# HGRN level products by predicated copies, two affine maps on ScalarE, and a two-pass norm in a one-core hybrid trunk layer

## The chip, the cores and the metric

The kernel runs on one core of one Trainium2 chip. The metric is the device time of that core in microseconds (us). A core has TensorE (PE in the profile; PEld is its weight load), VectorE (DVE), ScalarE (ACT), GpSimd (POOL) and the DMA queues, most of them issued by SyncE (SP). Each engine works through its own instructions in a fixed order and waits on semaphores for the others.

## The reference, cut to what matters

One layer of a bidirectional trunk is computed for a prompt of 256 rows and a sample of 2048 rows, 1024 columns each:

```
h = rms_norm(x) * (1 + scale1) + shift1
r,k,v,w,a,g | xb,gb | q,f,iv,og = split(h @ w_in)          # three groups of heads
mix = [rwkv7(r,k,v,w,a,g), rglru(xb,gb), hgrn2(q,f,iv,og)]  # each forward and backward
x = x + gate1 * (mix @ w_out)
x = x + gate2 * (silu(conv3(h2 @ w_gate)) * (h2 @ w_up)) @ w_down,   h2 = modulated rms_norm(x)
```

Two parts bear on the change. RWKV-7 needs, for each direction, the decay `exp(-exp(-softplus(-wl) - 0.5))`, which the kernel gets as the exponential of a running sum of `-c * (tanh(wl/2) + 1)`, and the keys `k * (1 + (a - 1) * k_a)`. HGRN2 works in chunks of 64 rows and needs, in every chunk, the 64 x 64 matrix `att[t, s] = sum_k q_t k_s exp(b_t - b_s)`, for s up to t forward and for s from t on backward.

## The kernel before, in words

All 2304 rows are held transposed, in nine pieces of 256 rows (PC). A first phase, `dense1`, takes five sections (four of two pieces, then one of one). For each section it goes through 29 column blocks of `w_in`, and each block is 8 x 3 matmuls: operands are split in two fp32r parts, hi and lo (L370, L371), and `mm3` (L374 to L376) sums three of the four products. In section 0 the weights are split on the spot and kept in DRAM; later sections load them back.

The small work is written as generators in six lanes. After every half block the main loop advances each lane by a fixed rate: lane 0 takes the RWKV jobs (`rw_job`, 40 of them: 5 sections x 4 pairs of heads x 2 directions), lane 2 HGRN and RG-LRU jobs (`hg_job`, 9), lane 3 the norm of the next section (`norm1`) and, behind it, further columns of the modulation. Lane 3 is run at high priority. That gives an order and a priority to each instruction; when the program is built, a planner with its own idea of durations then lays out the order of each engine, and adds the semaphores. After that nothing is reordered. A second phase does the prompt's output projection and MLP while the last jobs run, a third the same for the sample, with the backward scans beside it.

`norm1` (L452) takes a section in blocks of 128 rows, 14 blocks for the four later sections: load a block (tile x, one buffer, shared with the modulation's columns), Square with a row sum on ScalarE (L460), a reciprocal root by thirteen small VectorE instructions (`rsqrt`, L189 to L202, on a 128 x 1 column of tile nss), scaling on VectorE (L463), eight transposes (L469), modulation (L473) and a store to DRAM.

`rw_job` (L535) gets the decay's logarithm from a tanh on ScalarE (L551) and an affine map on VectorE (L553), then a scan (L558). The second tanh (L562) gives `a`; L572 forms (tanh + 1) * kk from it, L573 maps it affinely in place with two per-partition scalars, and L574 multiplies by k. L567 and L568 are exponentials, L577 to L580 the four products that go out, and L581 copies the chunk's last decay (128 x 8).

`hg_job` (L842) builds att for eight chunk-heads as one tile A (128 x 512, tile hA): first the diagonal (L900), then for the block sizes 1, 2, 4, 8, 16 and 32 a product on TensorE into PSUM (two for size 2, so seven in all). The product is right only where its level's 0/1 mask holds. So VectorE multiplies it by the mask into tile hl, which has one buffer (L923), and GpSimd adds hl to A (L924). L928 and L933 move decays on for the next level. The masks of the levels and the diagonal do not overlap and together cover all 64 x 64 places.

Of the kernel before, what the change touches and what calls it, by code (L numbers as in the profile page):

```python
# [10 lines left out]
F32 = mybir.dt.float32  # L11
# [90 lines left out]
def build(tc, a, o):  # L102
# [36 lines left out]
    eps = cst.tile([128, 4], F32, name="eps")  # L139
    for i, v in enumerate((RMS_EPS, GN_EPS, 1e-12, 0.0)):  # L140
        V.memset(eps[:, i:i + 1], v)
# [249 lines left out]
    def mt(tag, shape=(128, PC), bufs=1, dt=F32):  # L391
        return mp.tile(list(shape), dt, tag=tag, bufs=bufs, name=tag)
# [59 lines left out]
    def norm1(sec, n, xpool, xb):  # L452

        for b in range(2 * n):
            c = cond_of(sec + b // 2)
            ss = mt("nss", (128, 3), 2)
            x = xpool.tile([128, 1024], F32, tag="x", bufs=xb, name="x")
            SY.dma_start(x, xrows(None, sec * PC + b * 128, 128))
            jk = hp.tile([128, 1024], BF16, tag="hx", bufs=HXB, name="jk")
            S.activation(jk, x, AF.Square, accum_out=ss[:, 0:1])  # L460
            yield
            rsqrt(ss[:, 1:2], ss[:, 0:1], ss[:, 2:3], 1.0 / 1024, RMS_EPS)
            V.tensor_scalar_mul(x, x, ss[:, 1:2])  # L463
            yield
            for k4 in range(2):
                pt = ps("mm", [128, 4, 128], 2)
                for i in range(4):
                    k = 4 * k4 + i
                    T.transpose(pt[:, i, :], x[:, k * 128:k * 128 + 128], ident)  # L469
                hx = hp.tile([128, 4, 128], F32, tag="hx", bufs=HXB, name="hx")  # L470
                for i in range(4):
                    k = 4 * k4 + i
                    V.tensor_scalar(hx[:, i, :], pt[:, i, :], A1[:, k, c:c + 1], mod[:, k, c:c + 1],  # L473
                                    op0=ALU.mult, op1=ALU.add)
                SY.dma_start(dH[SI[sec]][4 * k4:4 * k4 + 4, :, b * 128:b * 128 + 128].rearrange("k p t -> p k t"), hx)
                yield
        h32s[sec] = True
# [57 lines left out]
    def rw_job(sec, n, p, d):  # L535
# [16 lines left out]
        yield  # L552
        V.tensor_scalar(th, th, -HALF_C, -HALF_C, op0=ALU.mult, op1=ALU.add)  # L553
        B = mt("t2", (128, 512))[:, :W]
# [17 lines left out]
        V.scalar_tensor_tensor(na, ta, 1.0, kk, op0=ALU.add, op1=ALU.mult)  # L572
        V.tensor_scalar(ta, ta, kah[:, p:p + 1], ka1[:, p:p + 1], op0=ALU.mult, op1=ALU.add)  # L573
        V.tensor_tensor(ta, ta, k, op=ALU.mult)  # L574
# [5 lines left out]
        V.tensor_tensor(AR[:, :, 1, :], c3(r), in_, op=ALU.mult)  # L580
        V.tensor_copy(WC[d][si][:, :, p:p + 1], ep[:, :, 64:65] if d == 0 else ep[:, :, 0:1])  # L581
        yield
# [260 lines left out]
    def hg_job(q, sec):  # L843
# [52 lines left out]
        A = mt("hA", (128, 8, 64))  # L896
        fA = A.rearrange("p c t -> p (c t)")
        G.tensor_tensor(j2(Ks), j2(Ks), qs, op=ALU.mult)
        pt = headsum(Ks)
        V.tensor_tensor(A, c8(pt), C[:, C_DG:C_DG + 64].unsqueeze(1).to_broadcast([128, 8, 64]), op=ALU.mult)  # L900
        yield
        for li, b in enumerate(LEVELS):
# [9 lines left out]
            else:  # L912
# [7 lines left out]
                terms = [(pt.rearrange("p c t -> p (c t)"), C_LV + 64 * li)]  # L920
            for pt, mo in terms:
                tl = mt("hl", (128, 8, 64))
                V.tensor_tensor(tl, c8(pt), C[:, mo:mo + 64].unsqueeze(1).to_broadcast([128, 8, 64]), op=ALU.mult)  # L923
                G.tensor_tensor(A, A, tl, op=ALU.add)  # L924
            gq = g[:, 0:2 * (Wg + 1)].rearrange("p (s r) -> p s r", s=2)[:, ::-1, 0:Wg:2]
# [867 lines left out]
```

## Time and profile before

| | |
|---|---|
| median of 3 runs | 4045.39 us (4037.32 to 4047.43) |
| profiled execution | 4042.86 us, of which the span from first to last instruction is 4041.1 us |
| mean granted TensorE clock | 0.949 of full speed |
| busy: PE, PEld | 3710.6 us (92%), 3095.8 us (77%) |
| busy: DVE, ACT, POOL | 2677.7 us (66%), 1483.4 us (37%), 1296.0 us (32%) |
| HBM | 472.69 MB read, 162.06 MB written, 157 GB/s over the span |

The page cuts the span into 40 slices. In the first fifteen, which are `dense1`, PE is busy 6 to 9 tenths and DVE 5 to 8; from slice 24 on PE is at 9 or more nearly throughout. In the groups below, a row gives busy microseconds, a mean in nanoseconds, and the idle time just before with what ended it; L numbers are lines of the kernel.

### The profile page before, as it was taken

The numbers are of one execution on the slowest core, as the hardware profiler recorded it, in microseconds if no ns is written. First come the engines' busy times: TensorE is split into PE (matmuls) and PEld (weight loads), VectorE is DVE, ScalarE is ACT, GpSimd is POOL, SyncE is SP. The second block draws the span as 40 slices with busy tenths as digits, with TensorE's granted clock in tenths as the row PEclk, the third lists the DMA queues.
The fourth block names the chain that finished last, engine by engine and source line by source line (L and its number), as shares of the span: only waits on it lengthen the run. The fifth ranks groups of instructions, "written<-read, shape, count | busy, mean of one in ns | idle before, by whom it ended". The sixth has DMA issues, their size and how long they took to land.

```text
span 4041.1 us, 75063 instructions
## 1 busy us (share of the span) xinstructions
PE 3710.6 (92%) x29752; PEld 3095.8 (77%) x29752; DVE 2677.7 (66%) x5203; ACT 1483.4 (37%) x2643; POOL 1296.0 (32%) x871
## 2 busy tenths in 40 slices
PE   6988999989999987799877999999989999999998
PEld 3766777767767775677765888888778999988998
DVE  5587888688668678966788754444764433376666
ACT  3445335334543545333333222222332222243333
POOL 2561132213023131233453333333333333333233
PEclk8999999989999887889999999999999999999999
DMA  7988977667776887654645322222512222242332
GB/s 243 300 253 247 273 206 231 223 197 224 245 213 204 256 258 216 195 159 145 187 129 175 108 85 84 76 78 71 170 57 78 70 64 63 63 141 79 91 93 84
DMA packets 766949, 639.69 MB, mean 158 GB/s; under 512 B 246970, under 2 KB 647686, under 8 KB 765574
## 3 DMA queue, kind: packets, MB, share of 16 engines
q1 hardware_dynamic: 734198, 600.66, 48.9%
q10 hardware_dynamic: 32400, 34.22, 2.7%
q8 instruction: 235, 3.85, 0.4%
q14 instruction: 116, 0.95, 0.1%
HBM read 472.69 MB, written 162.06 MB: 157 GB/s over the span
## 4 chain that ended last, share of the span: by engine, by line
PE 43%; DVE 9%; DMA 4%; issue 2%; POOL 1%; ACT 1%; SPq 0%; ACTq 0%; DVEq 0%; POOLq 0%
PE mm L374 6%; PE mm L376 5%; PE mm L375 5%; PE xh L374 5%; PE xh L376 5%; PE xh L375 5%; DVE raw L1452 1%; DVE x L1476 1%; PE e L374 1%; PE e L375 1%; DMA raw<-in_ffn_w_down 1%; DVE tm L1530 1%; PE e L376 1%; PE o L375 1%; PE o L374 1%
## 5 line engine op out<-in xcount | busy, mean ns | idle before, releaser
L371 POOL TENSOR_TENSOR wlo<-raw,whi 128x1024 fp32r<-128x1024 f32 x273 | 667.3, 2446 | 956.3 <-ACT whi L370 713.7
L374 PE MATMUL mm<-hhi,whi 128*128 128x512 f32 (+2 forms) x2224 | 815.6, 367 | 33.8 <-DVE hx L473 8.8
L375 PE MATMUL mm<-hlo,whi 128*128 128x512 f32 (+2 forms) x2224 | 802.0, 361 | 8.4 <-DVE hlo L293 5.6
L376 PE MATMUL mm<-hhi,wlo 128*128 128x512 f32 (+2 forms) x2224 | 798.7, 359 | 3.0 <-POOL wlo L371 3.0
L370 ACT CAST whi<-raw 128x1024 fp32r<-128x1024 f32 x333 | 348.7, 1048 | 739.2 <-PE mm L376 287.1
L374 PEld LDWEIGHTS mm<-hhi,whi 128*128 128x128 f32 x2224 | 438.0, 197 | 94.0 <-DVE hx L473 10.7
L375 PEld LDWEIGHTS mm<-hlo,whi 128*128 128x128 f32 x2224 | 438.7, 197 | 53.5 <-DVE hlo L293 6.4
L376 PEld LDWEIGHTS mm<-hhi,wlo 128*128 128x128 f32 x2224 | 437.9, 197 | 48.2 <-POOL wlo L371 3.8
L371 POOL TENSOR_TENSOR alo<-gs,ahi 128x384 fp32r<-128x384 f32 (+1 forms) x154 | 151.8, 986 | 439.3 <-ACT ahi L370 430.6
L374 PE MATMUL xh<-hhi,whi 128*128 128x384 f32 (+1 forms) x824 | 274.9, 334 | 4.0 <-ACT hhi L370 4.0
L375 PE MATMUL xh<-hlo,whi 128*128 128x384 f32 (+1 forms) x824 | 272.8, 331 | 5.3 <-DVE hlo L371 3.4
L376 PE MATMUL xh<-hhi,wlo 128*128 128x384 f32 (+1 forms) x824 | 273.5, 332 | 0.0
L1640 DVE SCALAR_TENSOR_TENSOR gs<-xh,vec,gs 128x378 f32<-128x378 f32 (+1 forms) x103 | 60.8, 590 | 313.6 <-ACT gs L1636 313.6
L1476 DVE TENSOR_TENSOR x<-mm,x 128x512 f32<-128x512 f32 x218 | 148.8, 686 | 109.9 <-PE mm L376 107.8
L1476 DVE TENSOR_TENSOR x<-xh,x 128x512 f32<-128x512 f32 x220 | 150.6, 686 | 76.5 <-PE xh L376 74.2
L1452 DVE TENSOR_TENSOR raw<-raw,g 128x1024 f32<-128x1024 f32 x98 | 133.0, 1358 | 72.3 <-DMA raw<-in_ffn_w_down 65.7
L1646 DVE SCALAR_TENSOR_TENSOR gs<-fsg,gs 128x384 f32<-128x384 f32 (+1 forms) x154 | 122.8, 797 | 62.5 <-ACT fsg L1645 62.2
L374 PEld LDWEIGHTS xh<-hhi,whi 128*128 128x128 f32 x824 | 156.3, 190 | 7.5 <-ACT hhi L370 4.6
L746 POOL COPY gm<-ar 64x256 f32<-64x256 f32 x120 | 57.4, 478 | 326.0 <-PE c L791 267.0
L375 PEld LDWEIGHTS xh<-hlo,whi 128*128 128x128 f32 x824 | 156.2, 190 | 7.5 <-DVE hlo L371 3.7
L376 PEld LDWEIGHTS xh<-hhi,wlo 128*128 128x128 f32 x824 | 156.4, 190 | 0.8
L924 POOL TENSOR_TENSOR hA<-hA,hl 128x512 f32<-128x512 f32 x63 | 101.0, 1602 | 171.6 <-DVE hl L923 167.9
(613 smaller groups left out, 8614.9 us busy)
## 6 DMA issues: line engine op xcount, KB each, us to landing
whi<-dW SPq DMA_DIRECT2D x116, 512.0 KB
wlo<-dW SPq DMA_DIRECT2D x116, 512.0 KB
raw<-in_ffn_w_gate SPq DMA_DIRECT2D x88, 512.0 KB
raw<-in_ffn_w_up SPq DMA_DIRECT2D x88, 512.0 KB
raw<-in_ffn_w_down SPq DMA_DIRECT2D x88, 512.0 KB
raw<-in_w_out SPq DMA_DIRECT2D x40, 512.0 KB
dAR<-AR SPq DMA_DIRECT2D x32, 512.0 KB
araw<-in_ada_w SPq DMA_DIRECT2D x32, 512.0 KB
```

The source lines that it names most:

```text
L370: S.copy(hi, raw)
L371: e.tensor_tensor(lo, raw, hi.bitcast(F32), op=ALU.subtract)
L374: T.matmul(out, whi, xhi, start=first, stop=False)
L375: T.matmul(out, whi, xlo, start=False, stop=False)
L376: T.matmul(out, wlo, xhi, start=False, stop=last)
L746: G.tensor_copy(gm[H[h], :, h, 0:64], ar[H[h], :, 0, :])
L924: G.tensor_tensor(A, A, tl, op=ALU.add)
L1452: V.tensor_tensor(raw, raw, g[f].unsqueeze(1).to_broadcast([128, 2, 512]), op=ALU.mult)
L1476: V.tensor_tensor(x1b[:, FS[f]], pt, x1b[:, FS[f]], op=ALU.add)
L1530: V.tensor_scalar(t[:, 128 * i:128 * i + 128], pt[:, 128 * i:128 * i + 128], A2[:, k, c:c + 1], mod[:, 24 + k, c:c + 1], op0=ALU.mult, op1 ...
L1640: V.scalar_tensor_tensor(gv[:, :, 1:rw], pv[:, :, 0:rw - 1], cw(0), gv[:, :, 1:rw], op0=ALU.mult, op1=ALU.add)
L1646: V.scalar_tensor_tensor(gs[:, :w], sg[:, :w], 1.0, gs[:, :w], op0=ALU.add, op1=ALU.mult)
```

## The change

Three edits, in three nested functions, and one constant column for a bias.

```diff
-    for i, v in enumerate((RMS_EPS, GN_EPS, 1e-12, 0.0)):
+    for i, v in enumerate((RMS_EPS, GN_EPS, 1e-12, -HALF_C)):
         V.memset(eps[:, i:i + 1], v)
...
     def norm1(sec, n, xpool, xb):
+        ss = mt("nss", (128, 3, 4), 1)
+        def rows(b):
+            x = xpool.tile([128, 1024], F32, tag="x", bufs=xb, name="x")
+            SY.dma_start(x, xrows(None, sec * PC + b * 128, 128))
+            return x
+        for b in range(2 * n):
+            x = rows(b)
+            jk = hp.tile([128, 1024], BF16, tag="hx", bufs=HXB, name="jk")
+            S.activation(jk, x, AF.Square, accum_out=ss[:, 0, b:b + 1])
+            yield
+        rsqrt(ss[:, 1, :2 * n], ss[:, 0, :2 * n], ss[:, 2, :2 * n], 1.0 / 1024, RMS_EPS)
         for b in range(2 * n):
             c = cond_of(sec + b // 2)
-            ss = mt("nss", (128, 3), 2)
-            x = xpool.tile([128, 1024], F32, tag="x", bufs=xb, name="x")
-            SY.dma_start(x, xrows(None, sec * PC + b * 128, 128))
-            jk = hp.tile([128, 1024], BF16, tag="hx", bufs=HXB, name="jk")
-            S.activation(jk, x, AF.Square, accum_out=ss[:, 0:1])
-            yield
-            rsqrt(ss[:, 1:2], ss[:, 0:1], ss[:, 2:3], 1.0 / 1024, RMS_EPS)
-            V.tensor_scalar_mul(x, x, ss[:, 1:2])
+            x = rows(b)
+            V.tensor_scalar_mul(x, x, ss[:, 1, b:b + 1])
             yield
...
-        V.tensor_scalar(th, th, -HALF_C, -HALF_C, op0=ALU.mult, op1=ALU.add)
+        S.activation(th, th, AF.Identity, scale=-HALF_C, bias=eps[:, 3:4])
...
-        V.tensor_scalar(ta, ta, kah[:, p:p + 1], ka1[:, p:p + 1], op0=ALU.mult, op1=ALU.add)
+        S.activation(ta, ta, AF.Identity, scale=kah[:, p:p + 1], bias=ka1[:, p:p + 1])
...
-        V.tensor_copy(WC[d][si][:, :, p:p + 1], ep[:, :, 64:65] if d == 0 else ep[:, :, 0:1])
+        S.copy(WC[d][si][:, :, p:p + 1], ep[:, :, 64:65] if d == 0 else ep[:, :, 0:1])
...
+        def put(pt, mo):
+            m = C[:, mo:mo + 64].bitcast(I32).unsqueeze(1).to_broadcast([128, 8, 64])
+            V.copy_predicated(A, m, c8(pt))
         G.tensor_tensor(j2(Ks), j2(Ks), qs, op=ALU.mult)
-        pt = headsum(Ks)
-        V.tensor_tensor(A, c8(pt), C[:, C_DG:C_DG + 64].unsqueeze(1).to_broadcast([128, 8, 64]), op=ALU.mult)
+        put(headsum(Ks), C_DG)
...
-            for pt, mo in terms:
-                tl = mt("hl", (128, 8, 64))
-                V.tensor_tensor(tl, c8(pt), C[:, mo:mo + 64].unsqueeze(1).to_broadcast([128, 8, 64]), op=ALU.mult)
-                G.tensor_tensor(A, A, tl, op=ALU.add)
+            for term in terms:
+                put(*term)
```

The diagonal and the seven products are now written straight into their places of A by VectorE, with the mask as predicate; there is no multiplication, no tile between and no addition. In `rw_job` the two affine maps and the small copy are ScalarE's. `norm1` loads the section's blocks once for the sums of squares, takes one reciprocal root for all (128 x 4), loads them a second time, and goes on as before. The number of times a job hands back to the main loop is the same in each.

## Rows read from the trace of the kernel before

**Rows 1.** Busy time by stage: PE, PEld, DVE, ACT, POOL, granted clock, DMA share, GB/s.
```profile
0.00:1500.00 1500.00, 1346.33 (x12847) 1029.10 (x12849) 1105.74 (x2369) 659.51 (x1227) 426.75 (x312) 0.94 0.78 238
1500.00:2200.00 700.00, 575.75 (x5897) 469.71 (x5891) 547.18 (x1061) 271.25 (x506) 241.60 (x170) 0.88 0.59 175
2200.00:4041.00 1841.00, 1788.49 (x11020) 1597.01 (x11016) 1024.82 (x1773) 552.60 (x912) 627.68 (x389) 0.98 0.29 87
```

**Rows 2.** Waits of PE in the first 1500 us: total, times, longest.
```profile
PE mm L267 <- DMA adaw<-in_ada_w: 15.0, 4, 5.4
PE x L587 <- DVE BK L577: 14.3, 9, 3.4
PE c L781 <- DVE uv L776: 9.1, 5, 3.0
PE mm L374 <- DVE hx L473: 8.8, 5, 3.0
...
PE mm L407 <- ACT araw L405: 6.7, 4, 2.4
```

**Rows 3.** Busy time in four slices of 100 us, columns as in Rows 1.
```profile
700.00:800.00 100.00, 95.49 (x888) 72.63 (x887) 61.95 (x150) 39.25 (x72) 17.21 (x18) 0.97 0.73 236
800.00:900.00 100.00, 81.67 (x789) 60.96 (x790) 85.39 (x201) 36.88 (x69) 20.57 (x17) 0.88 0.66 189
...
1000.00:1100.00 100.00, 95.95 (x950) 71.62 (x950) 72.99 (x175) 54.50 (x104) 7.70 (x11) 0.98 0.78 241
...
1200.00:1300.00 100.00, 92.06 (x955) 70.55 (x955) 84.48 (x175) 33.51 (x70) 35.06 (x24) 0.93 0.67 203
```

**Rows 4.** The masked products (L923) in two of these slices: DVE busy alone.
```profile
700.00:800.00 100.00, 0.00 (x0) 0.97 0.73 236
800.00:900.00 100.00, 4.76 (x7) 0.88 0.66 189
```

**Rows 5.** The chain's pieces around 1644 us: start, duration, what.
```profile
1644.04 0.43 PE mm L375
...
1645.93 0.23 PE mm L375
```

**Rows 6.** GpSimd's adds (L924) in the first 1500 us: POOL busy alone.
```profile
0.00:1500.00 1500.00, 100.95 (x63) 0.94 0.78 238
```

**Rows 7.** Timeline, three of these adds and VectorE beside them: start, duration, what.
```profile
208.53 1.87 POOL L924 TENSOR_TENSOR hA<-hA,hl 128x512 f32<-128x512 f32 x1 [3.98 <-DVE hl L923]
208.57 0.68 DVE L928 TENSOR_TENSOR hK<-hK,hg 128x512 f32<-128x512 f32 x1
...
212.67 1.75 POOL L924 TENSOR_TENSOR hA<-hA,hl 128x512 f32<-128x512 f32 x1
...
213.20 1.51 DVE L553 TENSOR_SCALAR t<-t 128x512 f32<-128x512 f32 x1
...
216.68 1.67 POOL L924 TENSOR_TENSOR hA<-hA,hl 128x512 f32<-128x512 f32 x1 [2.25 <-DVE hl L923]
...
217.11 1.79 DVE L578 TENSOR_TENSOR AR<-kk,ep 128x512 f32<-128x512 f32 x1
```

**Rows 8.** Two lines' instructions in ns: min, median, max.
```profile
L553 DVE TENSOR_SCALAR t<-t x40: 274/427/1506, 119.6 to 1593.1; 128x512 f32<-128x512 f32 x32, 128x256 f32<-128x256 f32 x8
L578 DVE TENSOR_TENSOR AR<-kk,ep x40: 408/692/1814, 124.8 to 1595.1; 128x512 f32<-128x512 f32 x32, 128x256 f32<-128x256 f32 x8
```

**Rows 9.** VectorE's groups that the change touches.
```profile
L923 DVE TENSOR_TENSOR hl<-xh,C 128x512 f32<-128x512 f32 x63 | 43.0, 683 | 24.4 <-PE xh L870 14.0 <-PE xh L919 7.6 <-POOL hA L924 2.4
L573 DVE TENSOR_SCALAR t<-t,kah,ka 128x512 f32<-128x512 f32 (+1 forms) x40 | 32.5, 813 | 0.4
L553 DVE TENSOR_SCALAR t<-t 128x512 f32<-128x512 f32 (+1 forms) x40 | 20.3, 507 | 38.6 <-ACT t L551 38.5
L581 DVE COPY WC<-ep 128x8 f32<-128x8 f32 (+1 forms) x40 | 11.4, 286 | 0.1
L463 DVE TENSOR_SCALAR x<-x,nss 128x1024 f32<-128x1024 f32 x14 | 10.5, 750 | 0.3
```

**Rows 10.** All work on the norm's statistics (tile nss): DVE busy.
```profile
0.00:1600.00 1600.00, 44.49 (x196) 0.93 0.77 237
```

**Rows 11.** ScalarE's groups nearest to the added instructions.
```profile
L562 ACT ACTIVATE t<-x,a0h 128x512 f32<-128x512 f32 (+1 forms) x40 | 25.5, 639 | 7.3 <-PE x L547 6.5 <-ACT t L568 0.7
L238 ACT ACTIVATE cth<-vec 128x8 f32<-128x8 f32 x2 | 0.3, 200 | 3.6 <-DVE vec L182 3.6
```

**Rows 12.** Waits of ScalarE in the first 1600 us: total, times, longest.
```profile
ACT ep L567 <- DVE t L558: 63.6, 32, 6.3
...
ACT jk L460 <- DMA x<-in_x_sample: 23.6, 8, 7.1
```

More of the change, by code (lines that the diff above doesn't have):

```diff
@@ L896, in hg_job @@
         A = mt("hA", (128, 8, 64))
-        fA = A.rearrange("p c t -> p (c t)")
+        def put(pt, mo):
+            m = C[:, mo:mo + 64].bitcast(I32).unsqueeze(1).to_broadcast([128, 8, 64])
+            V.copy_predicated(A, m, c8(pt))
         G.tensor_tensor(j2(Ks), j2(Ks), qs, op=ALU.mult)
-        pt = headsum(Ks)
-        V.tensor_tensor(A, c8(pt), C[:, C_DG:C_DG + 64].unsqueeze(1).to_broadcast([128, 8, 64]), op=ALU.mult)
+        put(headsum(Ks), C_DG)
         yield
```

## Prediction

> **What bounds the kernel now.** I read the stages first. From 2200 us on PE is busy 1788 of 1841 us at a granted clock of 0.98: that part is TensorE's, and nothing in the change reaches it. All the touched jobs run in the first 1600 us. There, up to 1500 us, PE is busy 1346 us, so it idles 154 us, and its clock is 0.94 [rows 1]. A clock below 1 means stretches at the lower of two rates: one matmul of mm3 follows another after 0.43 us at 1644 us and after 0.23 us at 1646 us, that is, at 1.2 and at 2.4 GHz [rows 5]; what PE did before is that it had just stood still for a weight split. At 0.94 the 1346 busy microseconds hold 0.06 x 1346 = 81 that full clock would save, so at most 154 + 81 = 235 us can be won in this stage, and a microsecond less of idling is worth up to 235 / 154 = 1.53.
>
> Then the waits of PE. Apart from the first loads (15.0 us) the longest three are on VectorE: 14.3 for the RWKV products, 9.1, and 8.8 for the norm's modulation; the longest on ScalarE is 6.7 [rows 2]. Each is short (2 to 3 us) and there are many: PE meets a result that is a little late, again and again. The reader should take from these rows that VectorE is what is late, though nothing there is one big hole.
>
> The slices say the same. Without HGRN products (700, 1000) DVE is busy 62.0 and 73.0, PE 95.5 and 96.0, clock 0.97 and 0.98. With them (800, 1200; seven products in slice 800 and none in 700 [rows 4]) DVE is busy 85.4 and 84.5, PE 81.7 and 92.1, clock 0.88 and 0.93 [rows 3]. Lost time of PE per slice, idle plus (1 - clock) x busy, is on average 6.7 us without and 13.1 + 0.095 x 86.9 = 21.4 us with. So 17.5 us more of DVE go with 14.7 us more lost: a slope of 0.84 (two slices against two, and HGRN brings more than DVE work, so it is an upper bound).
>
> **The change, part by part.**
>
> *Adds on GpSimd.* 63 adds go, 101 us of POOL, 1.60 us each [rows 6]. POOL itself is no bound (427 of 1500 us, rows 1). What counts is VectorE: an instruction that reads two SBUF operands, or a plain SBUF-to-SBUF map, that meets a GpSimd add runs on until the add is over. Of three adds in the timeline, the first came while VectorE was at work, and the add took the delay (1.87 us, the VectorE product its usual 0.68); the second stretched L553 to 1.51 us, the third L578 to 1.79 us [rows 7], against medians of 0.43 and 0.69 [rows 8]. That is (0 + 1.08 + 1.10) / 3 = 0.73 us of VectorE per add, 63 x 0.73 = 46 us. Bounds: none, or all 101 us.
> The Trainium skill says of this ("SBUF — State Buffer", SBUF: two separate sides) that whoever starts first takes the shared port pair for its whole instruction and the other fully blocks. The trace agrees in kind; read as if VectorE always lost, it would put the price at the upper end, 101 us, but in rows 7 the add is the one that waits in one case of three.
>
> *Products.* 63 masked products and 9 for the diagonal become 72 predicated copies with the same PSUM source and the same mask. A product takes 0.683 us [rows 9]. No predicated copy stands in the trace. It might take as long, or, if it works at half rate because it also has to mind what is in A, 2 x 0.683: between no change and 72 x 0.683 = +49 us; a gain of the same order can't be excluded by a row, but it reads no less. I take no change, since source, mask and output have the size of the nearest row. The copies of one A are in order on one engine, so what fell to the add (waiting for POOL's other work, and hl's single buffer, 2.4 us of VectorE waits) goes too.
>
> *Affine maps and copy.* VectorE loses L573 (32.5), L553 (20.3) and L581 (11.4): 64 us [rows 9]. ScalarE gains 80 maps; the nearest row, a tanh with a pointer bias over the same shapes, has 0.64 us, so 51 us, and 40 small copies at 0.20 make 8 [rows 11]: 59 us on 660 of 1500 [rows 1]. The first map follows a tanh on the same engine and only moves the hand-over to VectorE one step later (VectorE already waits there, 38.5 us in all [rows 9]). The second is worse: L573 stood between two VectorE instructions; now ScalarE waits for L572 (it overwrites what L572 reads) and L574 waits for ScalarE. Behind the waiting map stand, on ScalarE, the casts of L370 and the evacuations of mm; VectorE has L577's, L578's and L580's products to do meanwhile. The price as a wait lies between nothing and what the same job shows at its exponential, 63.6 us over 32 times, 2.0 us each [rows 12]. I take the low end for VectorE's side and charge ScalarE's side below.
> The Trainium skill ("ScalarE: Activation LUTs", Rules for kernel authors) would keep multiply-and-add on VectorE. By that page's figures (What ACT_TABLE_LOAD costs) I estimate 0.80 us for the map with two pointer operands and 0.71 for the other at 512 columns, which would make the 59 us some 65; on this kernel VectorE's own row, 813 ns for L573, shows no advantage left.
>
> *Norm.* 14 reciprocal roots become 4. Work on nss takes 44.5 us, of which 10.5 is the scaling [rows 9, 10]; 34 x 10/14 = 24 us go. (I take an instruction on 128 x 4 to be as short as one on 128 x 1; were it four times as long, nothing would be won here.) Added are 14 loads of 512 KB, 7.3 MB; at the stage's 238 GB/s that is 31 us of a DMA system that is busy 0.78 of the time [rows 1]. PE's waits on DMA end with the first loads [rows 2], so I count the loads as hidden by the matmuls; uncovered they would cost those 31 us. They queue on SP with the weights and the jobs' stores, 14 issues more. One thing turns: ScalarE's Square used to absorb the late block (23.6 us of waits, 8 times [rows 12]); in the second pass VectorE's scaling meets it. I charge 8 us to VectorE (a third; bounds 0 and 24). The norm is done well before its section needs it: the first pass adds four loads and Squares to it, some 4 x 8 us at the longest wait seen (7.1 us) plus a Square, in a section of some 300 us (1500 by five), which the slower lanes fill.
>
> *Sum.* VectorE: -46 - 64 - 24 + 8 = -126 us of 1106. From below, PE's idling shrinks in proportion to VectorE's busy time, 126/1106 of 154 = 18 us. From above, slope 0.84: 106 us. The two are far apart and I take their geometric middle, 44: the slope is inflated by HGRN's own chains, the proportion ignores that late results pile up and that idling costs clock as well. Against it ScalarE's 59 us (9% more): proportional to all of PE's idling 14 us; ScalarE ends fewer and shorter of these waits than VectorE [rows 2], so I take 5. Net -39. The profiled execution took 4042.9 us, so 4004; it lies 2.5 us under the median of 4045.4, and 4005 is what I write for the median to come.
>
> **The rivals.**
>
> *The gain stays hidden (about 4040).* PE's order was laid out once; if the waits on VectorE are mostly true dependences, as L587 after the last of a job's products, or if the 31 us of loads come out, the relief is idle time on VectorE. For it: each wait is short and PE waits for many lines. Against it: the slices with a quieter VectorE have PE at 95 to 96.
>
> *ScalarE becomes the late one (about 4070).* Forty second maps each stand at the head of ScalarE's queue until VectorE has done L572. With the exponential's 2.0 us and 0.64 us of work that holds ScalarE 40 x 2.64 = 106 us, and each evacuation behind it holds a PSUM buffer of mm. At the same slope of 0.84, 89 us if all of it reaches PE, 67 at three quarters; less the 44 won, that is +23 to +45, so 4066 to 4088. It decides from one half on, 0.84 x 53 = 44. For it: ScalarE's longest wait is of just this kind [rows 12]. Against it: mm has two buffers and a block takes some 10 us (29 in a section of about 300), so a hold of 2.6 us is mostly bridged.
>
> *All of the slope (about 3941).* VectorE's 126 us come out at 0.84, less ScalarE's 5. For it: slices 800 and 1000. Against it: 235 us is all there is, and part of it is loads at the start.
>
> *The planner's new order is worse by itself (some 4060).* Shorter jobs by its own durations move every engine's order in the first 2200 us; the second stage with its clock of 0.88 [rows 1] is the fragile one, and a few per cent of its 700 us are 20. Nothing in the rows speaks for a sign.
>
> **How the numbers follow.** Forecast, 3975 to 4032: 0.61. Whole slope: 0.09. Hidden: 0.18. ScalarE late: 0.08. Worse order: 0.04. A measurement of this kernel tells about 0.3%, 12 us, from no change. So faster 0.61 + 0.09 = 0.70, the same 0.18, slower 0.12. Copies at half rate would cost 49 x 44/126 = 17 us, still within the forecast (4022). The range goes from 3950, which leaves out most of the whole-slope case, to 4052, which leaves out the slower two.
>
> **What would show it.** Right: no add on GpSimd with tile hA; VectorE's busy time up to 1500 us near 980; L578, L580 and L928 seldom above 0.7 us; a predicated copy near 0.68 us; PE over 90 in the slices with HGRN, and clock above 0.95 in the stage. Wrong: a copy near 1.3 us; ScalarE's waits for L572 of more than 2 us each, with PE waiting for casts or evacuations; VectorE waiting for x loads for more than 24 us; or the first stage shorter while the second, up to 2200 us, takes it back.

## The result, and the profile after

The changed kernel takes 3988.98 us (median of 4 runs, 3979.92 to 3993.76) against 4042.61 us for the kernel before on the same chip: a ratio of 0.9865, 95% interval 0.9841 to 0.9889, or 54 us less. The forecast was 4005, in a range from 3950 to 4052. The profiled execution took 3979.92 us with a span of 3978.1, so it is the fastest of its runs, 63 us under the profiled execution of before.

The stages of after, to be laid beside [rows 1] (columns as there):

```profile
0.00:1500.00 1500.00, 1367.36 (x13588) 1049.63 (x13590) 1058.27 (x2263) 755.39 (x1426) 324.49 (x257) 0.96 0.82 253
1500.00:2200.00 700.00, 573.56 (x5496) 470.51 (x5493) 549.78 (x1056) 253.84 (x465) 258.64 (x177) 0.88 0.55 163
2200.00:4041.00 1841.00, 1735.35 (x10672) 1549.99 (x10671) 961.31 (x1637) 532.27 (x873) 607.83 (x374) 0.99 0.28 84
```

The first stage is denser (PE 1346 to 1367 busy at a clock of 0.96 instead of 0.94) and holds more of the work; the last only ends earlier. To see where the time was won, one needs a point of the work, not of the clock. I take the first gate product of the prompt's MLP on ScalarE, L1636 before and L1643 after. Times of these instructions in ns (min, median, max), then first and last start; before, then after:

```profile
L1636 ACT ACTIVATE gs<-mm,vec x8: 557/558/565, 1705.1 to 1843.3; 128x256 f32<-128x256 f32 x8
```
```profile
L1643 ACT ACTIVATE gs<-mm,vec x8: 558/560/567, 1643.8 to 1778.3; 128x256 f32<-128x256 f32 x8
```

So 61.3 of the 63 us are won before this point, called the gate from here on. Busy time up to the gate, before and after (columns as in [rows 1]):

```profile
0.00:1705.10 1705.10, 1498.27 (x14638) 1147.76 (x14639) 1279.96 (x2810) 754.31 (x1416) 460.41 (x343) 0.92 0.77 235
```
```profile
0.00:1643.80 1643.80, 1468.75 (x14583) 1126.58 (x14584) 1177.72 (x2544) 810.15 (x1531) 353.98 (x280) 0.93 0.81 248
```

VectorE is busy 102 us less, ScalarE 56 more, GpSimd 106 less. PE's idle time falls from 206.8 to 175.1 us (the stretch less its busy time), and its busy time falls by 29.5 us at a clock of 0.93 instead of 0.92: idling and the clock share the gain, roughly half and half (after shows 55 matmul records fewer before this point, worth some 5 us of the busy time). Behind the gate, where nothing was edited, the profiled execution of before takes 2336.0 us and that of after 2334.3.

The longest of PE's waits up to 1500 us (total, times, longest), for [rows 2]:

```profile
PE mm L267 <- DMA adaw<-in_ada_w: 16.2, 4, 5.0
PE x L552 <- ACT t L557: 11.5, 2, 10.8
PE mm L374 <- ACT whi L370: 7.9, 3, 3.7
PE e L761 <- DVE gm L755: 7.0, 3, 4.7
PE c L780 <- ACT mv L775: 6.5, 3, 3.2
```

The three waits on VectorE that stood behind the first loads (14.3, 9.1, 8.8) have left the top; one of 7.0 us is the longest left. Adding up the whole lists up to the gate, PE waits 37 us less for VectorE (114.7 before, 77.7 after), 11 us more for ScalarE (53.4, 64.1), and 2 us less for loads directly (25.6, 23.6). So the late results that went are VectorE's.

A wait on ScalarE has come in, most of it a single one of 10.8 us, on a tanh (L557). What ScalarE and VectorE did before it (start, duration, what, idle before and its releaser):

```profile
378.25 1.06 ACT L463 ACTIVATE jk<-x 128x1024 bf16<-128x1024 f32 x1 [8.20 <-DMA x<-in_x_sample]
...
383.18 0.23 DVE L1339 COPY hl<-hgS 128x128 f32<-128x128 f32 x1 [8.19 <-DMA dLA<-hl]
...
386.08 1.28 ACT L557 ACT_TABLE_LOAD   x1 [6.21 <-DVE nss L196]
...
388.11 0.79 PE L552 MATMUL x<-la,lrha 128*128 128x512 f32 x1 [10.83 <-ACT t L557]
```

The norm's Square waits 8.2 us for its rows, VectorE waits 8.2 us for a DMA that stores tile hl, and the tanh then waits for VectorE. So this wait goes back mostly to DMA, and not to the maps moved to ScalarE. Four slices of after, for [rows 3]:

```profile
700.00:800.00 100.00, 88.55 (x830) 66.28 (x827) 59.42 (x127) 34.12 (x63) 21.32 (x19) 0.90 0.67 214
800.00:900.00 100.00, 94.58 (x927) 71.59 (x927) 74.70 (x170) 43.31 (x83) 14.54 (x14) 0.91 0.76 219
...
1200.00:1300.00 100.00, 93.98 (x1139) 73.48 (x1136) 74.03 (x156) 45.13 (x93) 24.19 (x23) 0.96 0.78 228
...
1400.00:1500.00 100.00, 88.41 (x1269) 76.05 (x1267) 76.82 (x185) 62.79 (x134) 13.94 (x16) 0.94 0.86 276
```

In slices 800 and 1200 PE is at 94, where it had 82 and 92, with VectorE at 74 to 75 instead of 85. But HGRN's copies have moved too: slice 700, which had no product before, now holds four copies, as many as slice 800, and PE is at 88.6 there; slice 1400 holds eight, with PE at 88.4. So single slices do not show a size; the stage as a whole does.

VectorE's groups up to 1600 us (busy, mean ns, idle before and its releasers), for [rows 9], and two lines in ns (min, median, max), for [rows 8]; L584 is L578 of before:

```profile
L907 DVE COPY_PREDICATED hA<-C,xh 128x512 f32<-128x512 int32 x72 | 52.5, 730 | 24.0 <-PE xh L876 14.0 <-PE xh L928 9.4
...
L584 DVE TENSOR_TENSOR AR<-kk,ep 128x512 f32<-128x512 f32 (+1 forms) x40 | 25.9, 649 | 9.7 <-ACT ep L573 9.6
...
L469 DVE TENSOR_SCALAR x<-x,nss 128x1024 f32<-128x1024 f32 x14 | 12.6, 901 | 15.2 <-DMA x<-in_x_sample 15.1
```
```profile
L907 DVE COPY_PREDICATED hA<-C,xh x72: 708/728/751, 180.1 to 1437.6; 128x512 f32<-128x512 int32 x72
...
L584 DVE TENSOR_TENSOR AR<-kk,ep x40: 409/684/1366, 124.9 to 1535.2; 128x512 f32<-128x512 f32 x32, 128x256 f32<-128x256 f32 x8
```

The copy costs 0.73 us, hardly more than the product that it replaces. L584's maximum fell from 1814 to 1366 ns, but its neighbours still run to 2541 (L586) and 2774 ns (L585; L579 of before had 2007), so one line's maximum says little; the sum over all lines stands with the experiments. Work on the norm's statistics up to 1600 us, for [rows 10], fell from 44.5 to 21.3 us:

```profile
0.00:1600.00 1600.00, 21.28 (x66) 0.94 0.82 251
```

The new work on ScalarE, as groups, for [rows 11]:

```profile
L579 ACT ACTIVATE t<-t,ka,kah 128x512 f32<-128x512 f32 (+1 forms) x40 | 30.8, 771 | 25.4 <-DVE t L578 20.4 <-DVE ep L572 4.1 <-ACT mv L835 0.4
L559 ACT ACTIVATE t<-t,eps 128x512 f32<-128x512 f32 (+1 forms) x40 | 27.3, 681 | 2.7 <-DMA tt<-dTT 1.7
...
L587 ACT COPY WC<-ep 128x8 f32<-128x8 f32 (+1 forms) x40 | 7.9, 197 | 0.1
```

Together 66 us. For 512 columns the medians of L579 and L559 are 0.81 and 0.72 us. L579's wait for VectorE's L578 is the one that the ScalarE rival lived on; among ScalarE's waits up to 1600 us (total, times, longest) it stands like this, for [rows 12]:

```profile
ACT ep L573 <- DVE t L564: 49.3, 31, 6.8
...
ACT t L579 <- DVE t L578: 20.4, 15, 5.8
```

### The profile page after: what moved, and what is told of

It is laid out like the page before. It is cut to its first block, busy times and chain, and to the rows that moved or that the text cites. A ratio compares the mean times of both kernels' runs of the same rounds, so it can differ in the third digit from the quotient of the medians.

```text
span 3978.1 us, 74856 instructions
## 1 busy us (share of the span) xinstructions
PE 3676.3 (92%) x29752; PEld 3070.1 (77%) x29752; DVE 2569.4 (65%) x4953; ACT 1541.5 (39%) x2762; POOL 1191.0 (30%) x808
## 4 chain that ended last, share of the span: by engine, by line
PE 52%; DVE 14%; DMA 6%; ACT 3%; issue 3%; POOL 1%; SPq 1%; ACTq 0%; DVEq 0%; POOLq 0%
PE mm L374 7%; PE mm L376 7%; PE mm L375 7%; PE xh L374 6%; PE xh L375 5%; PE xh L376 5%; DVE raw L1459 2%; DVE x L1483 1%; DMA raw<-in_ffn_w_down 1%; DVE m L638 1%; DVE Dn L636 1%; PE e L374 1%; PE e L375 1%; PE e L376 1%; DVE tm L1537 1%
## 5 line engine op out<-in xcount | busy, mean ns | idle before, releaser
L371 POOL TENSOR_TENSOR wlo<-raw,whi 128x1024 fp32r<-128x1024 f32 x273 | 667.2, 2446 | 971.5 <-ACT whi L370 698.6
L374 PE MATMUL mm<-hhi,whi 128*128 128x512 f32 (+2 forms) x2224 | 798.6, 360 | 24.5 <-ACT whi L370 7.9
L375 PE MATMUL mm<-hlo,whi 128*128 128x512 f32 (+2 forms) x2224 | 785.4, 353 | 7.7 <-DVE hlo L293 5.6
L376 PE MATMUL mm<-hhi,wlo 128*128 128x512 f32 (+2 forms) x2224 | 784.9, 353 | 3.0 <-POOL wlo L371 1.8
L374 PEld LDWEIGHTS mm<-hhi,whi 128*128 128x128 f32 x2224 | 425.6, 192 | 83.8 <-issue 10.1
L375 PEld LDWEIGHTS mm<-hlo,whi 128*128 128x128 f32 x2224 | 426.2, 192 | 51.2 <-DVE hlo L293 6.3
L376 PEld LDWEIGHTS mm<-hhi,wlo 128*128 128x128 f32 x2224 | 426.0, 192 | 46.6 <-POOL wlo L371 3.0
L371 POOL TENSOR_TENSOR alo<-gs,ahi 128x384 fp32r<-128x384 f32 (+1 forms) x154 | 151.8, 986 | 419.5 <-ACT ahi L370 419.3
L371 POOL TENSOR_TENSOR t<-t,t 128x512 fp32r<-128x512 f32 (+1 forms) x40 | 52.9, 1323 | 359.7 <-ACT t L370 222.0
```

The lines of the kernel that those rows point to most:

```text
L371: e.tensor_tensor(lo, raw, hi.bitcast(F32), op=ALU.subtract)
L374: T.matmul(out, whi, xhi, start=first, stop=False)
L375: T.matmul(out, whi, xlo, start=False, stop=False)
L376: T.matmul(out, wlo, xhi, start=False, stop=last)
```

## The experiments

Theories that the expectations speak of. *VectorE*: the time comes from VectorE's shorter busy time, at one rate for all of it. *Chain*: it comes from A's chain over GpSimd (product, tile hl, add) being gone. *Port*: GpSimd instructions that read SBUF stretch VectorE's instructions, and the planner does not foresee it. *Queue*: GpSimd's adds cost by holding up what stands behind them on GpSimd. *Surprise*: such a stretch, called a stall here, costs more time than the same time of work that the planner knows. *Order*: a new set of instructions makes the planner lay the engines out anew, and that by itself moves the time. Each row gives the stretch up to the gate, columns as in [rows 1]; a single profile stands behind it, so I read differences of ten and more there. Behind the gate none of these kernels differs from the others in what it does, yet that part takes from 2318 to 2336 us in their profiled executions: so much goes by the order that the planner lays out, or by the single execution, and has nothing to do with the theory under test.

**Copies alone.** Before, with the predicated copies and nothing else.

```diff
-                V.tensor_tensor(tl, c8(pt), C[:, mo:mo + 64]..., op=ALU.mult)
-                G.tensor_tensor(A, A, tl, op=ALU.add)
+                put(*term)
...
```

> Only the predicated copies are taken over; the maps, the small copy and the norm are as before. Theory VectorE (what was won is VectorE time, and each microsecond of it brings some 0.43 us): 46 us less of port waits, 72 copies 0.045 us dearer, so 43 us of VectorE, some 18 us faster, about 4024. Theory chain (what was won is the HGRN job's own chain through GpSimd, whose queue stood 168 us for tile hl): nearly the whole gain is here, 40 us or more, 4003 or less. Theory order (any edit moves the planner's order, and the time with it): no relation to either, within 25 us of before on either side.

Measured: 3989.18 against 4043.86, ratio 0.9861 (0.9843 to 0.9878), 55 us less. This part alone is worth as much as the whole change.

```profile
0.00:1660.70 1660.70, 1480.68 (x14660) 1136.18 (x14661) 1224.15 (x2803) 757.02 (x1416) 356.88 (x280) 0.93 0.80 241
```

VectorE loses 56 us, the gate comes 44 us earlier. One common rate had foretold 4024: wrong. The chain theory had foretold 4003 or less; so far it stands.

**ScalarE's part alone.** The two maps and the small copy; the edit's middle one is shown.

```diff
...
-        V.tensor_scalar(ta, ta, kah[:, p:p + 1], ka1[:, p:p + 1], op0=ALU.mult, op1=ALU.add)
+        S.activation(ta, ta, AF.Identity, scale=kah[:, p:p + 1], bias=ka1[:, p:p + 1])
...
```

> Only the two affine maps and the small copy go to ScalarE. Theory VectorE: 64 us off VectorE, 27 us, less some 5 us for ScalarE's 69 us more: about 4020. Theory chain: nothing or a loss, 4042 to 4055, since the second map now crosses engines twice. Theory order: within 25 us of before on either side.

Measured: 4021.40, ratio 0.9939 (0.9924 to 0.9954), 22 us less. That is the figure of one common rate, 4020. But VectorE loses 50 us, nearly as many as with the copies, for less than half the gain.

```profile
0.00:1694.70 1694.70, 1487.94 (x14580) 1138.66 (x14581) 1229.77 (x2660) 809.16 (x1530) 454.74 (x343) 0.92 0.78 236
```

**The norm alone.** Two passes, one `rsqrt` per section.

```diff
...
+        rsqrt(ss[:, 1, :2 * n], ss[:, 0, :2 * n], ss[:, 2, :2 * n], 1.0 / 1024, RMS_EPS)
         for b in range(2 * n):
...
+            x = rows(b)
+            V.tensor_scalar_mul(x, x, ss[:, 1, b:b + 1])
```

> Only the norm in two passes. Theory VectorE: 24 us of reciprocal roots and 13 us of waiting for the Square gone, 17 us of waiting for loads and blocked scaling added: 20 us of VectorE, about 9 us faster, 4034. Theory chain: no change, 4042. If the 14 loads more were not covered: up to 31 us slower, 4073. Theory order: within 25 us of before on either side.

Measured: 4029.11, ratio 0.9956 (0.9939 to 0.9973), 15 us less, of which the gate shows 2.5.

```profile
0.00:1702.60 1702.60, 1493.24 (x14605) 1141.30 (x14605) 1243.83 (x2665) 750.20 (x1411) 451.40 (x343) 0.92 0.79 239
```

The three parts alone add up to 55 + 22 + 15 = 92 us; together they give 54. Up to the gate the gains do add up, 44 + 10 + 2.5 = 57 us against 61. What is missing lies behind it: there each single kernel is 7 to 10 us faster than before, and the whole change 2, with nothing edited in that part (and the whole change was profiled in its fastest run, 9 us under its median). VectorE's relief before the gate, on the other hand, does not add up: 56 + 50 + 36 = 142 us against 102.

**Copies, with GpSimd's adds back but tied to nothing.** After each copy GpSimd adds two constants into a tile that nobody reads. The chain stays gone, the reads of SBUF come back.

```diff
                 put(*term)
+                G.tensor_tensor(mt("hl", (128, W)), C[:, 0:512], C[:, 512:1024], op=ALU.add)
```

> As the kernel with the copies alone, but after each of the seven copies of a job GpSimd adds two blocks of constants (128 x 512) into a tile that nobody reads: the same 63 adds on the same port, with no tie to A. Theory VectorE: the port waits are back, 40 us or more of VectorE, and two thirds or more of what the copies alone won is lost: 4035 to 4042. Theory chain: the chain stays free, so what the copies alone won stays, within 6 us of that kernel.

Measured: 4035.86, ratio 0.9978 (0.9966 to 0.9991): 47 of the 55 us are lost again, so the chain theory falls, and what the port theory had foretold, 4035 to 4042, came. Up to the gate:

```profile
0.00:1712.80 1712.80, 1492.30 (x14580) 1144.21 (x14581) 1274.20 (x2788) 757.81 (x1415) 448.41 (x343) 0.92 0.77 233
```

VectorE, which got no instruction more, is busy 50 us more, and the gate is 52 us later. The adds as a group, then the timeline of VectorE beside two of them (start, duration, what):

```profile
L926 POOL TENSOR_TENSOR hl<-C 128x512 f32<-128x512 f32 x63 | 92.9, 1475 | 2.7
```
```profile
199.31 1.74 POOL L926 TENSOR_TENSOR hl<-C 128x512 f32<-128x512 f32 x1
...
199.82 1.78 DVE L580 TENSOR_TENSOR AR<-r,ep 128x512 f32<-128x512 f32 x1
```

L580 starts half a microsecond after an add and takes 1.78 us; in the kernel with memsets below, where nothing of GpSimd stands beside it, it took 0.68:

```profile
253.23 0.68 DVE L580 TENSOR_TENSOR AR<-r,ep 128x512 f32<-128x512 f32 x1
```

**Copies, with memsets on GpSimd.** As much of GpSimd's time, without a read.

```diff
                 put(*term)
+                tl = mt("hl", (128, W))
+                for _ in range(3):
+                    G.memset(tl, 0.0)
```

> The kernel with the copies alone (3989 us), and after each of the seven copies of a job GpSimd clears an idle tile (128 x 512) three times: as much GpSimd time as an add (3 x 0.5 us by the 0.98 us of a 128 x 1024 memset), in the same place of its queue, but it reads nothing. Theory port (the 47 us that idle adds took back were VectorE standing behind an add that reads SBUF): two thirds or more of the gain stays, under 4008, and the products of L928 and the small maps are not stretched by these memsets. Theory queue (what the adds cost is GpSimd's queue, with the splits for TensorE behind it): the gain goes as with the adds, 4030 to 4042.

Measured: 3973.16 against 4046.50, ratio 0.9822 (0.9802 to 0.9842). Nothing is lost. By the ratios it is even 16 us better than the copies alone; in the profiles 8 us of it lie before the gate and 9 behind it, where the two kernels do the same, and no run here gives a reason. Order is what is left, not shown.

```profile
0.00:1652.40 1652.40, 1466.48 (x14644) 1126.21 (x14645) 1220.48 (x2801) 756.53 (x1416) 453.56 (x469) 0.94 0.80 242
```
```profile
L928 POOL MEMSET hl<- 128x512 f32 x189 | 100.8, 533 | 8.4
```

GpSimd spends 101 us on memsets, VectorE's busy time stays (1220 against 1224). The timeline has both cases side by side, for one and the same line L932:

```profile
208.81 2.40 POOL L371 TENSOR_TENSOR wlo<-raw,whi 128x1024 fp32r<-128x1024 f32 x1
209.52 2.24 DVE L932 TENSOR_TENSOR hK<-hK,hg 128x512 f32<-128x512 f32 x1 [1.79 <-ACT hH L917]
211.14 2.86 POOL L928 MEMSET hl<- 128x512 f32 x5
211.68 0.74 DVE L901 COPY_PREDICATED hA<-C,xh 128x512 f32<-128x512 int32 x1
...
212.44 0.69 DVE L932 TENSOR_TENSOR hK<-hK,hg 128x512 f32<-128x512 f32 x1
```

Beside a split (L371), which reads two tiles, it takes 2.24 us and ends half a microsecond after it; beside memsets it takes 0.69. So it is the reads that do it, not GpSimd's being busy. The Trainium skill ("SBUF — State Buffer", Who interferes with whom) has the same rule: a VectorE instruction with two SBUF inputs contends with a GpSimd instruction that reads SBUF, not with one that only writes it.

**Copies, with the adds on VectorE.** The same 63 adds as planned work of VectorE.

```diff
                 put(*term)
+                V.tensor_tensor(mt("hl", (128, W)), C[:, 0:512], C[:, 512:1024], op=ALU.add)
```

> The kernel with the copies alone, and after each of the seven copies VectorE itself adds two blocks of constants into an idle tile: 63 x 0.68 = 43 us of VectorE work, as much as the port waits were, but known when the planner lays out the order. Theory every microsecond of VectorE counts the same: the gain goes as with the idle adds on GpSimd, 4030 or more. Theory surprise (a stall that the plan does not hold makes TensorE wait, work in the plan is mostly laid beside it): a loss of 10 to 25 us, 3999 to 4014.

Measured: 4005.68, ratio 0.9893 (0.9871 to 0.9915).

```profile
0.00:1681.50 1681.50, 1483.68 (x14668) 1136.29 (x14669) 1266.32 (x2864) 759.28 (x1421) 362.43 (x282) 0.93 0.79 238
```
```profile
L926 DVE TENSOR_TENSOR hl<-C 128x512 f32<-128x512 f32 x63 | 56.7, 901 | 6.1 <-POOL hVt L371 5.5
```

Against the copies alone VectorE's busy time rises by 42 us, not far from the 50 with GpSimd's adds, but the gate comes only 21 us later instead of 52, and the loss against the copies alone is 55 - 41 = 14 us instead of 47. So in this pair a microsecond of stall cost 47/50 = 0.93 us, a microsecond of planned work 14/42 = 0.33 (by the gate 52/50 and 21/42; the 14 is good to about 11 either way, and the kernel with GpSimd's adds was profiled in a run 8 us above its median). With order alone worth up to some 16 us, the two rates differ, but neither is known well.

The stall can also be added up from the traces: for each of VectorE's instructions up to the gate, what it took beyond the median of its kind (same operation, tiles and shape, over all kernels here but the null change; what took less counts as nothing). That gives 199 us before, 144 with the copies alone, 193 with GpSimd's idle adds, 144 with its memsets, 148 with the adds on VectorE, and 141 after. So nearly all that the copies took off VectorE was stretch, the idle adds brought it back, the memsets did not, and the adds on VectorE are work.

**A null change.** Before, with one tiny memset per HGRN job on VectorE, to see what a new layout does by itself.

```diff
...
+        V.memset(nul, 0.0)
```

> The kernel before with one memset of 128 x 8 on VectorE (0.06 us) at the start of each of the nine HGRN jobs: no work to speak of, but the planner lays out a different order. It measures what an order alone is worth. Theory order for the later stages (what the single edits won behind the first gate product of the prompt, 6 to 10 us, is order): the time from that product to the end, 2336 us before, moves by 5 to 10 us either way, and the whole by up to 12. Theory of a robust order: within 4 us of before everywhere.

Measured: 4045.04, ratio 0.9993 (0.9981 to 1.0005). Its gate is at 1706.3 us, 1 us later than before. An edit as small as this moves nothing. That says nothing on larger ones.

**Copies and norm.**

```diff
+                put(*term)
+        ss = mt("nss", (128, 3, 4), 1)
```

> The change without ScalarE's part: copies and the two-pass norm. Theory additive up to the first gate product of the prompt (44 us for the copies, 2.5 for the norm, 10 for ScalarE's part, 61 for all): that product at 1658 us, 10 us later than with the whole change, and the total between 3980 and 4000 by the order behind it. Theory saturation (once the copies are in, the rest is worth nothing): that product at 1660 with and without the norm, and the total as with the copies alone, 3989.

Measured: 3996.23, ratio 0.9880 (0.9860 to 0.9899), 50 us less, that is, 4 worse than the copies alone, within the intervals; the gate is 12 us later. Beside the copies the norm does not help. Both theories had the gate at 1658 to 1660; neither has a reason for 1672.

```profile
0.00:1672.40 1672.40, 1476.74 (x14603) 1133.02 (x14604) 1220.41 (x2664) 754.38 (x1415) 351.17 (x280) 0.93 0.80 243
```

VectorE's busy time is that of the copies alone within 4 us.

**Copies and ScalarE's part,** that is, the change without the norm.

```diff
+                put(*term)
+        S.activation(th, th, AF.Identity, scale=-HALF_C, bias=eps[:, 3:4])
```

> The change without the two-pass norm: copies and ScalarE's part. Theory additive up to the first gate product of the prompt (before 1705 us; 44 us for the copies, 10 for ScalarE's part): that product at 1651 us or earlier, total 3970 to 3985. If the norm's second loads cost in the whole change (copies with the norm were 7 us slower than copies alone), this one is some 10 us faster than the whole change, 3978. Theory saturation: as the copies alone, 3989.

Measured: 3972.36 against 4041.59, ratio 0.9819 (0.9794 to 0.9844), 69 us less. Here ScalarE's part is worth 15 us on top of the copies, and 20 at the gate, where the additive theory had 10. Against the whole change the kernel without the norm is 15 us faster; the two intervals just meet, and the gate shows 3 us of it.

```profile
0.00:1640.40 1640.40, 1465.32 (x14645) 1123.02 (x14646) 1184.31 (x2686) 813.38 (x1536) 356.72 (x280) 0.94 0.81 244
```

**The change, with more of GpSimd's reads on VectorE.** If a stall costs more than work, VectorE should take on GpSimd's products for the two smallest levels (L919), the splits of the head sums and the sum and product on Ks: 27, 76 and 18 instructions.

```diff
-            split(hi, lo, x)
+            split(hi, lo, x, V)
...
-        G.tensor_tensor(Ks, K[0], K[1], op=ALU.add)
+        V.tensor_tensor(Ks, K[0], K[1], op=ALU.add)
...
-                    G.tensor_tensor(blocks(P, b), qv, ..., op=ALU.mult)
+                    V.tensor_tensor(blocks(P, b), qv, ..., op=ALU.mult)
```

> The whole change, and GpSimd's remaining two-operand work of the HGRN and RWKV jobs also goes to VectorE: 27 products (L919 after), 67 splits for head sums (tiles hVt and t) and 18 products for the diagonal (hl). By the trace of the change these make VectorE run on for some 80 us behind GpSimd; done by VectorE itself they are 121 x 0.68 = 82 us of work in the plan. Theory surprise (a port wait costs its own length, planned VectorE work 0.3 of it): 80 won, 25 lost, 55 us faster than the change, about 3934. Theory every microsecond of VectorE counts the same: no difference, 3985 to 3993.

Measured: 3948.14 against 4041.59, ratio 0.9761 (0.9739 to 0.9784): 93 us less than before and some 40 less than the change.

```profile
0.00:1629.40 1629.40, 1467.71 (x14631) 1128.40 (x14632) 1175.02 (x2672) 815.30 (x1536) 172.56 (x159) 0.93 0.83 250
```

GpSimd lost half of its work, VectorE took it over, and VectorE's busy time is no longer for it (1175 against 1178): the stalls that went are as long as the work that came (by the reckoning above, stretch falls from 141 to 77 us). The gain was nearer to the 55 us of the surprise theory than to nothing. But the two profiled spans are 30.5 us apart (3978.1 and 3947.6), of which 14 lie before the gate; the other 16 lie behind it, where none of the moved instructions stands.

**Copies alone, with the same move.**

> The copies and the same move to VectorE, without ScalarE's part and the norm. Theory surprise: the same 55 us off the copies alone (3989), 3934, though VectorE is fuller by 64 us here and some of it may come back: 3934 to 3950. Theory every microsecond counts the same: 3989.

Measured: 3980.74, ratio 0.9849 (0.9825 to 0.9874): 61 us less than before, 6 better than the copies alone, which the intervals do not tell from nothing. A miss for the surprise theory, which had 3934 to 3950: stretch falls from 144 to 75 us, as much work comes in its place, and little is won.

```profile
0.00:1649.70 1649.70, 1475.62 (x14672) 1130.60 (x14673) 1219.29 (x2914) 756.14 (x1418) 176.28 (x161) 0.93 0.80 242
```

**The move without the norm.** As two above, with the old norm.

```diff
-        ss = mt("nss", (128, 3, 4), 1)
+            ss = mt("nss", (128, 3), 2)
+            rsqrt(ss[:, 1:2], ss[:, 0:1], ss[:, 2:3], 1.0 / 1024, RMS_EPS)
```

> The copies, ScalarE's part and the move of GpSimd's products and splits to VectorE, with the norm as it was (one load, fourteen reciprocal roots). Theory norm costs (its second loads and the scaling that waits for them cost 7 us beside the copies and 17 beside copies and ScalarE's part): some 12 us faster than the kernel with the norm in two passes (3948), 3931 to 3941. Theory order (the norm's sign is the planner's order, as it was 15 us faster alone): anywhere from 3935 to 3965, and sections 0 to 3 some 10 to 20 us later than with the two passes, as they were without the move.

Measured: 3946.80 against 4045.44, ratio 0.9767 (0.9741 to 0.9793): the same as with the new norm; the gate is 4 us earlier.

```profile
0.00:1625.50 1625.50, 1458.21 (x14620) 1118.46 (x14621) 1178.10 (x2795) 811.67 (x1536) 174.45 (x159) 0.95 0.81 246
```

So the norm's worth has no fixed sign: 15 us won alone, nothing or a little lost beside the copies, 15 lost beside copies and ScalarE's part (at the edge of the intervals), nothing beside the moved work. These two kernels, about 3947 us, are the best of all that ran.

## Why the prediction was right, and where its steps were not

**Place and direction: right.** VectorE was late, PE stood still and lost clock for it; 61 of 63 us were won where the touched jobs run, in idle time and in PE's clock, and PE's waits for VectorE fell by 37 us. A microsecond less of idling was worth more than the 1.53 taken as the most: 61.3 us came with 31.7 less of idling, or about 37 if the 55 matmuls fewer are missing records.

**The total: right by offsetting errors.** The sum was net 39 us, measured are 54. Its terms:

*Adds on GpSimd.* The stall was sized well: 46 us of VectorE's time were forecast. The copies alone measured 56, or 59 with the 72 x (730 - 683) ns = 3 us that the copies cost more than the products. What failed is the price. At the prediction's rate of 44/126 = 0.35 us per microsecond of VectorE, 46 would have given 16 us; 55 came. The two experiments with the adds put back point to the reason: stall 0.93, planned work 0.33. Both do the same copies and the same adds of constants; the engine of the adds differs, and so whether VectorE's time is planned work or a hold-up (the planner's order differs too). That a stall costs more because the planner does not foresee it is argued, not shown.

*Maps and copy.* ScalarE's part took 50 us off VectorE, not 64, and gave 22 alone, or 0.44 per microsecond; the forecast's 0.35 x 64 - 5 = 17 is near. The 5 us charged to ScalarE were too few: PE's waits for ScalarE up to the gate grew by 12 us with this part alone (53.4 to 65.9) and by 11 with the whole change, though not beside the copies (52.9). Part of what these lines took was stall (L553's mean is 507 ns, its median 427 [rows 8, 9]), and a stall lands on the next instruction instead of vanishing with the line. The stretch reckoned above bears this out in sum, not one by one: alone the copies, ScalarE's part and the norm take 55, 12 and 21 us of it away, together 58 instead of 88, and that is 30 of the 40 us by which VectorE's relief falls short (142 singly, 102 together). On ScalarE the maps cost 66 us, not 59; the nearest row was shorter. The Trainium skill's figures ("ScalarE: Activation LUTs", What ACT_TABLE_LOAD costs) had given estimates of 0.80 and 0.71 us at 512 columns and 65 us in all; medians of 0.81 and 0.72 agree, and were the better guide. The page's rule ("ScalarE: Activation LUTs", Rules for kernel authors) to keep such maps on VectorE would have cost 22 us here, small copy included.

*Norm.* The work on nss fell by 23.2 us, 24 were forecast, so an instruction on 128 x 4 is as short as one on 128 x 1. VectorE waits 15.1 us for the loads, inside the bounds of 0 and 24 and twice the 8 taken, and ScalarE's Square still waits 18.1 (23.6 before). PE has no new wait on a load itself, and the DMA share went from 0.78 to 0.82. But to read from this that loads are hidden is too simple, in the prediction as in the rows of after: PE's longest wait, 10.8 us, stands behind two engines that waited for DMA, one of them ScalarE with a Square of the norm. Whether the second loads made it is not shown. That the norm's relief would come out as time is what failed: beside the copies VectorE's busy time falls by 4 us only, and the change without the norm is some 15 us faster than with it, at the edge of the intervals. What gives the norm its sign is left open; loads that come late through other engines and the planner's order are both possible, and no run took them apart.

*Conversion.* 44 us were taken for 126; measured are 61 for 102 up to the gate, that is 0.60. The 44 was a middle between two figures far apart, so that it came near is luck in part. The slope of 0.84, which stood for the upper of the two, rested on two slices with HGRN. Between 200 and 1500 us before has five more with six or more products:

```profile
200.00:300.00 100.00, 89.69 (x765) 68.36 (x764) 82.78 (x109) 43.05 (x70) 61.62 (x33) 0.95 0.82 252
...
500.00:600.00 100.00, 90.36 (x1005) 69.90 (x1006) 82.32 (x152) 38.27 (x75) 37.20 (x28) 0.90 0.72 210
600.00:700.00 100.00, 96.43 (x1011) 71.05 (x1010) 84.92 (x180) 54.98 (x106) 25.64 (x20) 0.98 0.73 226
...
900.00:1000.00 100.00, 93.29 (x1094) 70.66 (x1090) 78.86 (x131) 41.91 (x84) 38.20 (x29) 0.97 0.74 221
...
1400.00:1500.00 100.00, 89.12 (x1031) 78.43 (x1032) 81.22 (x176) 49.57 (x107) 33.30 (x25) 0.91 0.82 259
```

By the prediction's own formula all seven lose 15.7 us on average at 82.9 of VectorE, against 6.7 at 67.5 without: a slope of 9.0 / 15.4 = 0.59, close to the 0.60 that came. The 0.35 was near what planned work brought (0.33 to 0.44) and far too low for stalls, which were over a third of the sum; the norm's term, which brought nothing beside the others, hid part of that. Nor are the two rates the whole law: the kernel with more work moved to VectorE trades stalls for work at no change of busy time and won 40 us on the change, but the same move on the copies alone won 6, where the two rates would have given more.

**The rivals.** *Hidden*: no, the gate moved. *ScalarE late*: the wait that it lived on is 20.4 us in 15 cases, 40 x 0.5 us instead of 40 x 2.0, and PE's waits for ScalarE grew by 11 us only, about as much as the one on a tanh (10.8 us) that goes back to DMA. *Whole slope*: the parts together gave 0.60 per microsecond, not 0.84, but the copies alone, 55 us for 56, beat 0.84, which had been called an upper bound. *Worse order*: an order can matter, since the part behind the gate took 2318 to 2336 us with nothing edited in it; the null change found nothing. Up to the gate, where 61 of the 63 us lie, the time went with VectorE's stretch in the kernels with adds and memsets, so order did not decide there.

**What would show it.** Of the signs named these came: no add with tile hA; the clock at 0.96 in the stage; copies at 0.73 for 0.68; the second stage takes nothing back. PE over 90 in the slices with HGRN came in nine of the twelve that hold copies, not in slices 300, 700 and 1400 (84.9, 88.6 and 88.4). Off is VectorE up to 1500 us, 1058 and not near 980, because a fixed window holds more of the work when the kernel is faster; up to the gate it is 102 of the 126 us. And stretched products remain (L585 up to 2774 ns), 141 us in all: GpSimd's splits and products still read SBUF, and with 121 of them moved to VectorE 77 us are left.

## What to carry to other kernels

Ask of each GpSimd instruction whether it reads SBUF beside a busy VectorE, and count its price as VectorE's stall, not as GpSimd's time: 63 idle adds cost 0.8 us of VectorE each here (50/63). In the one pair that compares them, a stall cost nearly its whole length and work in the plan a third to a half; another kernel, which traded 70 us of stall for about as much work, won 6, so take these as prices of this schedule. Price the two apart, and time parts alone and together, because here 92 us of single gains became 54. Compare two traces at a point of the work, not at a time: up to the gate the same gains were 57 and 61.

## What the runs showed of the hardware that was not expected

- A memset on GpSimd (0.53 us at 128 x 512) leaves VectorE's two-operand products at 0.69 us, while a split on GpSimd stretched one to 2.24.
- A predicated copy of 128 x 512 from PSUM under an int32 mask takes 0.73 us, 7% over the masked product (0.683).
- Moving half of GpSimd's work before the gate (354 to 173 us) onto VectorE left VectorE's busy time where it was (1178 to 1175): an instruction that takes a median of 1.29 us on GpSimd (L371, tile t) takes 0.69 on VectorE.
